# A four-layer decoder trunk: TensorE's instructions in the order of emission, with the emitter's clock and delays changed

## The chip, the cores and the metric

The kernel runs on 1 core of one Trainium2 chip. The metric is device time in microseconds (us) of one execution, and the median of the runs is what counts. TensorE does the products and transposes, VectorE, ScalarE and GpSimd the work between them, and SyncE issues most of the transfers.

## The reference

Four layers, 256 positions, model width 1024, all in float32. Layer i has mixer i mod 3 (so 0, 1, 2, 0) and a gated feed-forward block; each is wrapped in two RMS norms and added to x.

```python
for i in range(DEPTH):
    hn = rms_norm(x, norm_gains[i, 0])
    m = (diff_attention, stick_breaking_attention, sliding_window_sink_attention)[i % 3](hn, ...)
    x = x + rms_norm(m, norm_gains[i, 1])
    h = rms_norm(x, norm_gains[i, 2])
    f = (silu(h @ w_gate[i]) * (h @ w_up[i])) @ w_down[i]
    x = x + rms_norm(f, norm_gains[i, 3])
```

Each mixer projects hn to queries, keys and values, forms causal scores per head, turns them into weights (two softmaxes whose difference is taken; stick breaking; a softmax with a sink over a window of 128), applies them to the values and projects back. Mixers 0 and 2 rotate queries and keys by their positions (rope).

## The kernel before, in words

**Two streams.** The 256 positions are two streams of 128, stream 0 and stream 1. Both run the same layers, and stream 1 also needs the keys and values of stream 0. Every unit of weights (128 x 1024 floats, numbered in the order of use, `units`, L190 to L238) is used first by stream 0 and then by stream 1.

**Weights.** SyncE loads a unit into one of 4 staging tiles (`load_dma`, L242). ScalarE rounds it to `hi` and VectorE takes the rest as `lo` (`split`, L254); both are kept in a ring of 11. A product of float32 accuracy is three passes: hi by the high part of the activations, lo by the high part, hi by the low part. So a unit is six products of 512 columns for each stream in a mixer's projections, in the out-projection or in the feed-forward block.

**The parts of a layer.** `pre_norm` (L418) transposes x on TensorE and splits it into `xh` and `xl` (ScalarE, then VectorE, four slices for each half). `project` (L496) makes a chunk in a bank of PSUM: the first chunk of a mixer in an "acc" bank, the later ones in the one "mm" bank of the stream, which must have been read before the next chunk is written. In mixers 0 and 2 a chunk of queries or keys goes through `rope` (L510): two multiplications by VectorE that read the bank and an addition, then transposes (`tt`, `tq`, `tk`), then a copy by ScalarE. `scores` (L607 and L714) and `heads` (L807) make scores (`sc`), the weights, their transposes (`tw`, `ta`, `tpr`); `values` makes the output (`pv`), which mixer 0 normalises (`on`, with GpSimd's power) and transposes (`to`). `out_proj` (L483) is followed by `post_norm` (L457): squares by ScalarE, a power by GpSimd (`u_m`, then `r_m`), the update of x by VectorE. The feed-forward block (`ffn`, L871) has 11 chunks; a chunk's hidden values are turned by GpSimd copies and a transposing transfer (`hp`, `hq`, `hx` in `turn`, L891) and used by `down` (L880).

**What sets the order.** Each part is a generator. The `Emitter` (L42 to L155) runs them in turn and emits their instructions. It has a clock of its own, `t`, which only the products and transposes move on: `mm` (L374) adds the columns times `COLUMN_NS`, `transpose` (L386) four times as much for a column. A generator yields `("d", ns)` to be taken up again that much later by this clock, `("e", key)` to wait for an event of another part, and `("w",)` to ask for the next unit. Where nothing can be emitted, the clock jumps to the next due time. Small parts (transposes, scores, values) go first when they are due, then the two main generators.

What is emitted then goes to a scheduler that orders each engine's queue when the program is built. Instructions issued through `act`, `dve`, `pool` and `pe` (L187) are pinned behind what was emitted before them on their engine (`Start`, L172) as long as `on` is true. In the kernel before, all four are turned off at L933, when stream 1 has made its first norm of layer 0; from there on the scheduler chooses the order, and it may put a product of one part between two of another.

## Time and profile before

| | us |
|---|---|
| median of 3 runs | 1189.72 |
| lowest and highest | 1189.0, 1190.4 |
| the profiled execution's own time | 1188.92 |
| its span, first to last instruction | 1187.1 |

The profile is of one execution. Its page gives the busy time of each engine over the span; other views of the trace give it by stretch, list the instructions in order of time with start and length, and follow the chain of waits back from the end. A stretch is named by its start and end in us from the span's start. A group's name is what it writes, an arrow, and what it reads, with buffer numbers left out: `mm_f` is a feed-forward chunk, `mm_a010k` the key chunk of layer 0, stream 1, head group 0 (a for mixer 0, then layer, stream, group, part); `tp_q` are the transposes of x ahead of a feed-forward block and `tp_n` those ahead of a mixer; `acc` is an out-projection or down-projection. Layer 0's mixer lies from the start to 125, the feed-forward blocks of the four layers around 125 to 316, 420 to 610, 700 to 875 and 990 to the end.

### The profile page before, as it was taken

How to read it: one execution, taken by the hardware profiler on the slowest of the kernel's cores; microseconds unless marked ns; L12 is line 12 of the kernel's file. 1: busy time of each engine (PE TensorE's matmuls, PEld its weight loads, DVE VectorE, ACT ScalarE, POOL GpSimd, SP SyncE). 2: the span in 40 equal slices, each digit the busy share in tenths (PEclk: the TensorE clock that was granted, in tenths of full speed). 3: DMA queues.
4: the chain of work that ended last, by engine and by line, in shares of the span. 5: the costliest groups of instructions: out<-in, count | busy, mean ns of one | idle time of the engine just before them, and what ended most of it. 6: DMA issues, size and time to landing. Idle time of an engine off the chain costs nothing.

```text
span 1187.1 us, 16727 instructions
## 1 busy us (share of the span) xinstructions
PE 1165.9 (98%) x5868; PEld 958.5 (81%) x5868; DVE 784.4 (66%) x1217; ACT 651.9 (55%) x1197; POOL 214.3 (18%) x301
## 2 busy tenths in 40 slices
PE   8999999999999999999999999999999999999997
PEld 7787788888878878888888878888878788888886
DVE  7876665665847666665688666566586785666563
ACT  6665554444756655444476655445475565545442
POOL 2000132222200013222210013221210001322221
PEclk9999999999999999999999999999999999999999
DMA  7635467776743546777764246777765454677761
GB/s 280 212 122 161 146 189 222 209 213 199 239 143 125 178 143 185 216 219 209 200 214 141 90 147 195 213 210 210 207 214 154 137 175 128 177 213 214 208 194 41
DMA packets 184360, 216.41 MB, mean 182 GB/s; under 512 B 53074, under 2 KB 148436, under 8 KB 184276
## 3 DMA queue, kind: packets, MB, share of 16 engines
q1 hardware_dynamic: 183568, 215.00, 61.1%
q8 instruction: 46, 0.75, 0.3%
q10 hardware_dynamic: 708, 0.34, 0.1%
q14 instruction: 38, 0.31, 0.1%
HBM read 203.76 MB, written 1.05 MB: 173 GB/s over the span
## 4 chain that ended last, share of the span: by engine, by line
PE 90%; DVE 3%; ACT 3%; DMA 2%; issue 2%; POOL 1%; ACTq 0%; POOLq 0%; DVEq 0%; SPq 0%
PE mm_f L182 39%; PE acc_f L182 19%; PE acc_a L182 3%; PE mm_c L182 2%; PE acc_b L182 2%; PE sc_a L182 2%; PE acc_c L182 2%; DMA stage<-in_a_w_in_dram 1%; ACT hi L182 1%; DVE lo L182 1%; PE sc_c L182 1%; PE sc_b L182 1%; PE pv_a L182 1%; DVE x L182 1%; PE tp_q L182 1%
## 5 line engine op out<-in xcount | busy, mean ns | idle before, releaser
L182 DVE TENSOR_TENSOR lo<-stage,hi 128x1024 fp32r<-128x1024 f32 x378 | 459.7, 1226 | 162.0 <-ACT hi L182 159.9
L182 ACT ACTIVATE hi<-stage 128x1024 fp32r<-128x1024 f32 x378 | 394.9, 1056 | 163.3 <-PE mm_f L182 86.9
L182 PE MATMUL mm_f<-hi,xh_q 128*128 128x512 f32 x704 | 275.7, 392 | 1.5 <-ACT hi L182 1.5
L182 PE MATMUL mm_f<-lo,xh_q 128*128 128x512 f32 x704 | 274.2, 389 | 0.0
L182 PE MATMUL mm_f<-hi,xl_q 128*128 128x512 f32 x704 | 217.2, 390 | 0.4 <-DVE xl_q L182 0.4
L182 POOL COPY hp_f<-h_f 128x512 uint16<-128x512 uint16 x80 | 90.6, 1132 | 407.7 <-DVE h_f L182 393.7
L182 PEld LDWEIGHTS mm_f<-hi,xh_q 128*128 128x128 f32 x704 | 132.1, 188 | 30.5 <-ACT hi L182 3.2
L182 PEld LDWEIGHTS mm_f<-hi,xl_q 128*128 128x128 f32 x704 | 132.2, 188 | 28.7 <-DVE xl_q L182 1.2
L182 PEld LDWEIGHTS mm_f<-lo,xh_q 128*128 128x128 f32 x704 | 132.3, 188 | 26.9
L182 ACT ACTIVATE hTh_f<-hx_f 128x256 fp32r<-128x256 f32 x80 | 33.4, 418 | 166.8 <-POOL hx_f L182 166.8
L182 PE MATMUL acc_f<-hi,hTh_f 128*128 128x512 f32 x352 | 111.5, 393 | 1.2 <-ACT hTh_f L182 1.2
L182 PE MATMUL acc_f<-hi,hTl_f 128*128 128x512 f32 x352 | 109.8, 390 | 0.0
L182 PE MATMUL acc_f<-lo,hTh_f 128*128 128x512 f32 x352 | 109.8, 390 | 0.0
L182 DVE TENSOR_TENSOR hTl_f<-hx_f,hTh_f 128x256 fp32r<-128x256 f32 x80 | 33.9, 424 | 106.0 <-ACT hTh_f L182 106.0
L182 POOL COPY hx_f<-hq_f 128x512 uint16<-128x512 uint16 x80 | 81.0, 1013 | 85.6 <-DMA hq_f<-hp_f 85.1
L182 ACT ACTIVATE t_f<-mm_f,half_f 128x256 f32<-128x256 f32 x88 | 41.5, 472 | 74.4 <-PE mm_f L182 74.4
L182 PEld LDWEIGHTS acc_f<-hi,hTh_f 128*128 128x128 f32 x352 | 65.8, 188 | 15.5 <-ACT hTh_f L182 2.3
L182 PEld LDWEIGHTS acc_f<-lo,hTh_f 128*128 128x128 f32 x352 | 66.1, 188 | 13.8
L182 PEld LDWEIGHTS acc_f<-hi,hTl_f 128*128 128x128 f32 x352 | 66.0, 188 | 13.7
L182 DVE SCALAR_TENSOR_TENSOR t_f<-t_f,mm_f 128x256 f32<-128x256 f32 x88 | 36.8, 418 | 32.5 <-ACT t_f L182 32.4
L182 DVE SCALAR_TENSOR_TENSOR h_f<-t_f,hsq_f,mm_f 128x256 f32<-128x256 f32 x88 | 42.3, 480 | 2.9
L182 ACT ACTIVATE e_a<-sc_a,nm_a 128x128 f32<-128x128 f32 (+1 forms) x64 | 26.0, 420 | 17.0 <-DVE nm_a L182 16.9
(588 smaller groups left out, 1552.3 us busy)
## 6 DMA issues: line engine op xcount, KB each, us to landing
stage<-in_ffn_w_gate_dram SPq DMA_DIRECT2D x176, 256.0 KB, 3.0
stage<-in_ffn_w_up_dram SPq DMA_DIRECT2D x176, 256.0 KB, 3.3
stage<-in_ffn_w_down_dram SPq DMA_DIRECT2D x88, 512.0 KB, 4.4
stage<-in_a_w_in_dram SPq DMA_DIRECT2D x48, 512.0 KB, 4.4
stage<-in_b_w_in_dram SPq DMA_DIRECT2D x24, 512.0 KB, 4.1
stage<-in_a_w_out_dram SPq DMA_DIRECT2D x16, 512.0 KB, 3.5
stage<-in_c_w_in_dram SPq DMA_DIRECT2D x10, 512.0 KB, 4.4
gain<-in_norm_gains_dram SPq DMA_DIRECT2D x8, 512.0 KB, 4.3
```

What stands on the lines that cost most here:

```text
L182: i = call(*args, **kw)
```

## The change

TensorE's pin is no longer turned off, so its queue stands in the order of emission throughout; ScalarE, VectorE and GpSimd are let go at the same place as before. The clock's price of a column goes from 0.417 to 0.443 ns. The delays of nearly all parts are longer, and some yields are moved, taken out or added; two lines of them stand here for the table.

```diff
-COLUMN_NS = 1.0 / 2.4
+COLUMN_NS = 0.443
...
         def turned(chunk, g, which):
             t = rope(chunk, 8, *tabs[which], f"{name}{g}{which}")
-            yield ("d", 2000)
+            yield ("d", 2900)
...
-                    yield ("d", 3500)
+                    yield ("d", 1800 if step else 4200)
...
             split_rows(hT[c], slice(2 * (c % 2), 2 * (c % 2) + 2), t)
+            yield ("d", 1500)
             em.set((name, "h", c))
...
             if i == 0 and s:
                 scalars()
-                act.on = dve.on = pool.on = pe.on = False
+                act.on = dve.on = pool.on = False
...
             post_norm(s, acc, gain, f"m{i}{s}")
-            yield ("d", 4000)
+            yield ("d", 4600)
             gain = gain_of(i, 3)
             xn = pre_norm(s, 4 * i + 2, f"q{i}{s}")
-            yield ("d", 600)
+            yield ("d", 1200)
```

The instructions are the same ones before and after; only their order differs. In the rows below a name's last number is the buffer's and tells nothing; the number after hi or lo is the unit.

TensorE in layer 0, where the first query chunk of stream 0 (`t1_a000q`, after its rope) is transposed (`tt_a000q`). Before:

```order
L182 MATMUL mm_a000k_408<-hi_7_417,xh_n00_214 128x512
L182 MATMUL mm_a010q_359<-lo_3_293,xh_n01_297 128x512
L182 MATMUL mm_a000k_408<-lo_7_418,xh_n00_214 128x512
L182 MATMUL mm_a000k_408<-hi_7_417,xh_n00_214 128x512
L182 MATMUL mm_a000k_408<-lo_7_418,xh_n00_214 128x512
L182 MATMUL tt_a000q_402<-ident_164,t1_a000q_384 128x128 x4
L182 MATMUL mm_a000k_408<-hi_7_417,xl_n00_215 128x512 x2
```

After:

```order
L182 MATMUL mm_a010q_359<-hi_1_253,xl_n01_298 128x512 x2
L182 MATMUL mm_a000k_401<-hi_4_331,xh_n00_214 128x512
L182 MATMUL mm_a000k_401<-lo_4_332,xh_n00_214 128x512
L182 MATMUL mm_a000k_401<-hi_4_331,xh_n00_214 128x512
L182 MATMUL mm_a000k_401<-lo_4_332,xh_n00_214 128x512
L182 MATMUL mm_a000k_401<-hi_4_331,xl_n00_215 128x512 x2
L182 MATMUL tt_a000q_415<-ident_164,t1_a000q_384 128x128 x4
L182 MATMUL mm_a000k_401<-hi_5_368,xh_n00_214 128x512
```

The transposes stood among the products of unit 7; now they stand behind unit 4 of the key chunk, with units 0 and 1 for stream 1 ahead of that and units 5 to 7 behind. On VectorE, whose order is the same up to the rope's last addition, the splits of units 10 to 12 now stand ahead of the key chunk's rope, where only unit 10's stood within it; and later in this mixer `on_a000`, the normalisation of the first output, stands ahead of both multiplications that read the key chunk of stream 1, and before behind them.

TensorE at the entry of stream 1 into layer 0's feed-forward block (`x_1` is its x, `acc_a01` its out-projection, `mm_f00..` are chunks of stream 0 and `mm_f010` the first chunk of stream 1). Before:

```order
L182 MATMUL acc_a01_1_1326<-hi_31_1256,ol_a011_358 128x512
L182 MATMUL mm_f001_1469<-hi_39_1491,xh_q00_1362 128x512
L182 MATMUL mm_f001_1469<-lo_39_1492,xh_q00_1362 128x512
L182 MATMUL mm_f001_1469<-hi_39_1491,xh_q00_1362 128x512
L182 MATMUL mm_f001_1469<-lo_39_1492,xh_q00_1362 128x512
L182 MATMUL mm_f001_1469<-hi_39_1491,xl_q00_1363 128x512 x2
L182 MATMUL mm_f002_1661<-hi_42_1577,xh_q00_1362 128x512
L182 MATMUL acc_f00_0_1631<-hi_40_1514,hTh_f000_1557 128x512
L182 MATMUL tp_q01_0_1588<-ident_164,x_1_111 128x128 x4
L182 MATMUL acc_f00_1_1632<-hi_40_1514,hTh_f000_1557 128x512
L182 MATMUL tp_q01_1_1593<-ident_164,x_1_111 128x128 x4
L182 MATMUL mm_f010_1624<-hi_32_1275,xh_q01_1586 128x512
```

After:

```order
L182 MATMUL mm_f001_1469<-hi_39_1491,xl_q00_1369 128x512 x2
L182 MATMUL tp_q01_0_1588<-ident_164,x_1_111 128x128 x4
L182 MATMUL tp_q01_1_1593<-ident_164,x_1_111 128x128 x4
L182 MATMUL mm_f010_1624<-hi_32_1275,xh_q01_1586 128x512
L182 MATMUL mm_f010_1624<-lo_32_1276,xh_q01_1586 128x512
L182 MATMUL mm_f010_1624<-hi_32_1275,xh_q01_1586 128x512
L182 MATMUL mm_f010_1624<-lo_32_1276,xh_q01_1586 128x512
L182 MATMUL mm_f010_1624<-hi_32_1275,xl_q01_1587 128x512 x2
L182 MATMUL acc_f00_0_1635<-hi_40_1514,hTh_f000_1537 128x512
```

The products of units 42 and 40 that stood ahead of the transposes are behind them now; what stands ahead, up to `mm_f001`, is as before. GpSimd at the same place, before:

```order
L182 COPY hp_f000_1501<-h_f000_1465 128x512
L182 TENSOR_SCALAR u_m01_1549<-ssp_m01_1543 128x1
L182 COPY hx_f000_1559<-hq_f000_1503 128x2x256
L182 TENSOR_TENSOR r_m01_1550<-u_m01_1549,mhalf_126 128x1
L182 COPY hp_f001_1581<-h_f001_1570 128x512
```

After:

```order
L182 COPY hp_f000_1495<-h_f000_1465 128x512
L182 COPY hx_f000_1539<-hq_f000_1497 128x2x256
L182 TENSOR_SCALAR u_m01_1555<-ssp_m01_1549 128x1
L182 TENSOR_TENSOR r_m01_1556<-u_m01_1555,mhalf_126 128x1
L182 COPY hp_f001_1581<-h_f001_1570 128x512
```

The copy `hx_f000` stood between the two steps of stream 1's norm and now stands ahead of both. The entries of layers 1, 2 and 3 are changed in the same way on both engines.

TensorE in layer 2, where the keys of stream 0 are transposed (`tk_c20`, of `kd_c20` after its rope; `mm_c200` is the chunk that they come from, `mm_c201` the next). Before:

```order
L182 MATMUL mm_c201_6033<-lo_199_5963,xh_n20_5873 128x256
L182 MATMUL mm_c201_6033<-hi_199_5962,xl_n20_5874 128x256 x4
L182 MATMUL mm_c210_6087<-hi_196_5762,xh_n21_5999 128x256
L182 MATMUL tk_c20_5993<-ident_164,kd_c20_5984 128x128 x2
L182 MATMUL mm_c210_6087<-lo_196_5763,xh_n21_5999 128x256
```

After:

```order
L182 MATMUL mm_c200_5947<-lo_197_5785,xh_n20_5873 128x256
L182 MATMUL mm_c200_5947<-hi_197_5784,xl_n20_5874 128x256 x4
L182 MATMUL tk_c20_5993<-ident_164,kd_c20_5984 128x128 x2
L182 MATMUL tp_n21_0_6001<-ident_164,x_1_111 128x128 x4
L182 MATMUL tp_n21_1_6006<-ident_164,x_1_111 128x128 x4
L182 MATMUL mm_c201_6033<-hi_198_5816,xh_n20_5873 128x256
```

The key transposes stood behind the whole chunk `mm_c201` and the transposes of stream 1; now they stand directly behind the chunk that they need, ahead of both.

## The prediction

> **What bounds the kernel now.** First the page's busy times, then the busy time of each engine by stretch (columns: stretch, its length, then busy time and count of TensorE's matmuls, of its weight loads, of VectorE, ScalarE and GpSimd, the granted clock, the DMA share), cut at the mixers and feed-forward blocks.

> ```profile
> span 1187.1 us, 16727 instructions
> PE 1165.9 (98%) x5868; PEld 958.5 (81%) x5868; DVE 784.4 (66%) x1217; ACT 651.9 (55%) x1197; POOL 214.3 (18%) x301
> ...
> 0.00:40.00 40.00, 35.41 (x172) 29.13 (x173) 32.56 (x60) 25.80 (x39) 8.21 (x57) 1.00 0.79 272
> 40.00:125.00 85.00, 83.31 (x471) 67.03 (x470) 59.64 (x103) 52.75 (x146) 4.95 (x6) 1.00 0.48 150
> 125.00:150.00 25.00, 23.58 (x107) 18.62 (x106) 17.26 (x34) 14.56 (x30) 3.95 (x9) 1.00 0.52 158
> 150.00:290.00 140.00, 140.00 (x619) 116.04 (x618) 84.58 (x107) 65.79 (x87) 39.19 (x36) 1.00 0.74 208
> 610.00:700.00 90.00, 88.11 (x677) 75.12 (x676) 71.12 (x168) 60.05 (x167) 3.31 (x8) 1.00 0.44 141
> 875.00:990.00 115.00, 113.73 (x632) 92.37 (x631) 85.71 (x154) 71.48 (x185) 7.80 (x13) 1.00 0.49 155
> 1155.00:1187.10 32.10, 25.33 (x113) 20.35 (x111) 13.17 (x21) 7.36 (x16) 3.04 (x6) 0.95 0.12 42
> ```

> TensorE is the bound: it is idle for 1187.1 - 1165.9 = 21.2 us. Of that, 40.00 - 35.41 = 4.6 lie in the first 40 us and 32.10 - 25.33 = 6.8 in the last stretch, where the last norm and the store follow the last product; the order of TensorE's work shortens neither. So 9.8 us are left for a better order. Inside a feed-forward block (150 to 290) there is nothing: 140.00 of 140. Mixers 0, 2 and 3 hold 1.7, 1.9 and 1.3 us, and the entry of stream 1 into a feed-forward block (125 to 150) 1.4, four times over. The work itself is fixed, since the same instructions are issued before and after: what can change is only where TensorE waits. The chain of waits gives the pace, with which distances in an order become times:

> ```profile
> 172.11 8.16 PE mm_f L182 x36
> ```

> 36 products of 512 columns take 8.16 us, 0.227 each; six of them, one unit of weights for one stream, 1.36.

> An instruction at the head of TensorE's queue that waits holds all behind it, in either kernel. A place in the new order therefore costs the length of the chain on the other engines, by the trace, less the products that stand between. The five places where this comes out largest follow.

> **1. The first query transposes.** Rows of the timeline, start and length first:

> ```profile
> 19.74 0.39 PE L182 MATMUL mm_a010q<-hi,xh_n 128*128 128x512 f32 x1
> ...
> 25.82 0.68 DVE L182 TENSOR_TENSOR t_a000q<-mm_a000q,srq_a 128x512 f32<-128x512 f32 x1
> 26.43 1.21 DVE L182 TENSOR_TENSOR lo<-stage,hi 128x1024 fp32r<-128x1024 f32 x1
> 27.56 0.68 DVE L182 TENSOR_TENSOR t_a000q<-t_a000q 128x512 f32<-128x512 f32 x1
> ...
> 29.26 0.60 PE L182 MATMUL tt_a000q<-ident,t_a000q 128*128 128x128 f32 x4
> ```

> Stream 1's first products begin at 19.74, just behind the query chunk. Between that moment and the transposes the new order keeps 18 products (units 0 and 1 for stream 1, unit 4 for stream 0), so TensorE is at the transposes at 19.74 + 18 x 0.227 = 23.82. VectorE's order up to the rope's last addition is the same in both kernels, and that addition ends at 27.56 + 0.68 = 28.24. TensorE waits 4.4 us, give or take the 0.1 to 0.4 of a hand-over; before, products of units 2 to 7 filled this time. Nothing hides it, as the products that did stand behind the waiting transposes.

> **2. The value chunk behind it.** It uses the bank of the key chunk, which VectorE must have read twice. In the new order VectorE splits units 8 to 12 before the first of these two reads.

> ```profile
> 24.10 1.05 ACT L182 ACTIVATE hi<-stage 128x1024 fp32r<-128x1024 f32 x1
> ...
> 33.52 1.06 ACT L182 ACTIVATE hi<-stage 128x1024 fp32r<-128x1024 f32 x1 [0.40 <-DMA stage<-in_a_w_in_dram]
> ...
> 33.01 0.69 DVE L182 TENSOR_TENSOR t_a000k<-mm_a000k,srk_a 128x512 f32<-128x512 f32 x1
> ```

> The first of these ScalarE rows is unit 7, the second, five roundings later and waiting for its load, unit 12. VectorE's split of unit 12 can thus end at 33.52 + 1.06 + 1.21 = 35.8, the two reads at 0.6 each at 37.0. TensorE arrives at 28.3 + 0.4 + 30 x 0.227 = 35.5. That is 1.5 us; it is 0 if the loads run ahead during the first wait. Before, the second read ended at 33.70.

> **3. The middle of mixer 0.** VectorE's row of the normalised output of pv_a000 now stands ahead of both reads of the key chunk of stream 1, whose bank the value chunk needs.

> ```profile
> 52.30 0.28 ACT L182 ACTIVATE junk_a<-pv_a 128x128 bf16<-128x128 f32 x1 [1.16 <-PE pv_a L182]
> ...
> 54.80 0.69 DVE L182 TENSOR_TENSOR on_a<-pv_a,os_a 128x512 f32<-128x512 f32 x1 [1.16 <-POOL os_a L182]
> ...
> PE mm_a001k L182 <- DVE t_a001q L182: 0.7, 1, 0.7
> ```

> From pv_a's end (just before 52.30) to on_a's end is 3.2 us, and the two reads make it 4.4. Six products, 1.36, stand between: 3.0 us of wait. Before, TensorE waited 0.7 for a rope in this stretch (the last row: total, times, longest), which goes, and I take another 0.3 off for hand-overs beside it: +2.0, between 0 and 3.0.

> **4. Stream 1's entry into each feed-forward block**, four times.

> ```profile
> 141.81 0.39 PE L182 MATMUL acc_a<-hi,ol_a 128*128 128x512 f32 x1
> ...
> 143.02 0.30 POOL L182 TENSOR_SCALAR u_m<-ssp_m 128x1 f32<-128x1 f32 x1 [7.76 <-ACT junk_m L182]
> 143.38 0.75 POOL L182 COPY hx_f<-hq_f 128x512 uint16<-128x512 uint16 x1
> 143.92 0.49 PE L182 MATMUL mm_f<-hi,xh_q 128*128 128x512 f32 x1 [0.37 <-ACT hi L182]
> 144.07 0.57 POOL L182 TENSOR_TENSOR r_m<-u_m,mhalf 128x1 f32<-128x1 f32 x1
> ...
> 144.64 0.50 PE L182 MATMUL acc_f<-hi,hTh_f 128*128 128x512 f32 x1 [0.22 <-ACT hTh_f L182]
> 144.68 1.41 DVE L182 SCALAR_TENSOR_TENSOR x<-mg_m,r_m,x 128x512 f32<-128x512 f32 x2 [1.03 <-POOL r_m L182]
> ...
> 145.57 0.63 PE L182 MATMUL tp_q<-ident,x 128*128 128x128 f32 x4 [0.43 <-DVE x L182]
> ...
> 148.20 2.16 DVE L182 SCALAR_TENSOR_TENSOR xl_q<-tp_q,gains,xh_q 128x128 fp32r<-128x128 f32 x8
> ```

> Before: the last product of out-projection starts at 141.81, seven products later TensorE would be at 143.40. It waits three times, to 143.92, 144.64 and 145.57, and issues one product after each of the first two: 145.57 - 143.40 - 2 x 0.227 = 1.7 us lost. After: those two products are gone from here, so the transposes head the queue at 143.40. GpSimd's copy hx_f now stands ahead of u_m, so r_m starts at 143.32 instead of 144.07 and x comes 0.7 earlier: transposes at 144.85, a wait of 1.45. Their second half waits 0.35 for the second half of x. Then four products run, and the fifth needs xl_q, for which VectorE still has to do its queue behind x: in the trace 148.20 + 0.27 is 3.8 after x began, less the 0.3 of a subtraction that moved ahead gives 147.5, where TensorE stands ready at 146.86. Sum 1.45 + 0.35 + 0.65 = 2.45, or 0.75 more than before; four entries make +3.0. The copy that moved ahead costs nothing while its transfer has long landed; if that move gave nothing, x would come 0.7 later in all four, +5.8; if the three old waits merely merge into one, 0.

> **5. The keys of layer 2.** The transposes of the key chunk now stand right behind that chunk; before, 24 products of 256 columns, the transposes of stream 1 and a product lay between.

> ```profile
> 618.55 0.28 PE L182 MATMUL mm_c<-hi,xh_n 128*128 128x256 f32 x1
> ...
> 620.33 0.28 DVE L182 TENSOR_TENSOR t_c20k<-mm_c,srk_c 128x128 f32<-128x128 f32 x1
> ...
> 621.66 0.48 DVE L182 TENSOR_TENSOR kd_c<-t_c20k 128x128 f32<-128x128 f32 x2
> ```

> At 618.55 the chunk was done; the keys are ready at 622.14, and VectorE's order up to there is unchanged. The wait is 3.6 us, 2.4 if VectorE gets there without the split of 1.21 that stands between.

> **The rest.** Some six more places in mixers 2 and 3 have transposes directly behind a group that must be copied out of the same bank first. The gain elsewhere is at most the idle time of the three mixers, 1.7 + 1.9 + 1.3 = 4.9. The loss: such a copy and its subtraction cost

> ```profile
> 62.44 0.69 ACT L182 ACTIVATE oh_a<-to_a,gsub 128x512 fp32r<-128x512 f32 x1
> ...
> 63.66 0.74 DVE L182 SCALAR_TENSOR_TENSOR ol_a<-to_a,gsub,oh_a 128x512 fp32r<-128x512 f32 x1
> ```

> 0.69 + 0.74 = 1.4 each, at most 8 for six. I take the middle of -4.9 and +8, +1.5, as no row decides. SyncE's queue keeps its order but for one transposing transfer in layer 2, so the loads cost nothing by themselves; TensorE's longer delays between groups come free in the feed-forward blocks, where 140 of 140 us stay filled.

> **Sum.** 4.4 + 1.5 + 2.0 + 3.0 + 3.6 + 1.5 = +16.0 on the profiled execution's 1188.92 (its span of 1187.1 and 1.8 around it): 1204.9. The median of the three runs, 1189.72, lies 0.8 above that execution, so 1205.7, or 1206. With every term at its low end (4.0, 0, 0, 0, 2.4, -4.9) it is +1.5, 1191; at its high end (4.5, 1.5, 3.0, 5.8, 3.6, 8) +26.4, 1216.

> **The rivals.**

> *The clock falls during the long waits* (chance 0.12). In the trace TensorE never idles for long after the start, and at the start it is slow:

> ```profile
> 12.32 1.05 PE L182 MATMUL mm_a000q<-hi,xl_n 128*128 128x512 f32 x2
> 13.17 1.91 PE L182 MATMUL tp_n<-ident,x 128*128 128x128 f32 x8
> ```

> Two products take 13.17 - 12.32 = 0.85, twice the later pace. If waits 1 and 5 each brought back such a stretch, and it lasted as long as from there to 19.74 at most, each would cost up to half of 6.6 us, 3.3: 1206 + 6.6 = 1213. For it: two waits of 4 us, longer than any of before. Against it: the granted clock is given as 1.00 in all stretches but the last, so the page can't tell.
> [...]

> *The chains stay as long as in the trace everywhere* (0.15). The other engines' orders change little, so every rope that queued behind splits there may queue in the new order too, and hold TensorE at each group. All terms are then at their high ends, 1216, and with four ropes more at the 1.5 of place 2, 1222.

> *The waits of before go, and the new ones are short* (0.08): the other side, faster. VectorE's three operations for a rope are 0.68 each, 2.0 in all; where it is free at once, the distances in the new order cover them. Then terms 2, 3 and the rest turn into -4.9, and the entries gain their 0.7: 4 x (-0.7). It decides at the startup, in VectorE's addition: were it done by 23.8, wait 1 would be gone too, and with wait 5 halved the time is 1189.7 - 4.9 - 2.8 + 1.8 = 1183.8. Against it: VectorE's queue up to there is the same, and full, so I see no way to its being done before 28.

> *Nothing measurable* (0.05): the old and new waits cancel, 1190. It needs wait 1 and wait 5, 8 us, to be made good by 8 of the 9.8 idle us, which include the entries.

> The forecast has 0.60. **How the numbers follow.** 0.2%, about what a measurement of this kernel can tell from no change, is 2.4 us. The first, second and forecast cases are slower: 0.87; the third faster, 0.08; the fourth the same, 0.05. The range goes from 1194, leaving out the last two cases and the very lowest sum, to 1222, the end of the long-chain case.

> **What would show it.** In the profile after: TensorE waits on VectorE's t_a000q for some 4 us around 24, on kd_c for some 3.6 around 630, and on x before each tp_q of stream 1 for 1.4; mm_f in the blocks keeps 0.227. Wrong would be: no wait at tt_a000q or tk_c, or idle time of TensorE below 21 us. Products at twice the pace behind a wait would speak for the clock.

## The result, and the profile after

The changed kernel takes 1224.12 us (median of 4 runs, 1222.58 to 1225.83), the kernel before 1189.36 beside it: ratio 1.029, 95% interval 1.0277 to 1.0303. The profiled execution took 1222.58. Its page, the busy times:

```profile
span 1220.8 us, 16727 instructions
PE 1173.2 (96%) x5868; PEld 961.7 (79%) x5868; DVE 787.2 (64%) x1217; ACT 654.3 (54%) x1197; POOL 214.0 (18%) x301
```

TensorE is idle for 1220.8 - 1173.2 = 47.6 us, 26.4 more than before, and busy 7.3 us longer with the same 5868 instructions: together the 33.7 us by which the span has grown. The stretches show where (columns as before; the granted clock stands behind the five busy times):

```profile
0.00:40.00 40.00, 31.32 (x135) 25.24 (x136) 31.07 (x56) 24.21 (x33) 8.23 (x57) 0.91 0.80 281
40.00:137.00 97.00, 90.32 (x515) 72.94 (x514) 63.09 (x111) 56.49 (x152) 5.76 (x8) 0.98 0.40 122
162.00:300.00 138.00, 138.00 (x611) 114.26 (x610) 82.31 (x101) 64.30 (x84) 38.00 (x35) 1.00 0.72 205
627.00:716.00 89.00, 80.15 (x620) 68.56 (x621) 62.67 (x152) 54.81 (x156) 3.46 (x8) 0.96 0.33 108
905.00:1024.00 119.00, 111.90 (x616) 90.75 (x617) 83.33 (x150) 70.61 (x183) 7.38 (x12) 0.99 0.46 141
```

Inside a feed-forward block nothing is lost, as before. Mixers 0, 2 and 3 hold 6.7 (and 8.7 in the first 40 us), 8.9 and 7.1 us of idle time, and the clock is below 1 in just these stretches. The list of TensorE's waits (total, times, longest) gives them their names:

```profile
PE tp_q L182 <- DVE x L182: 5.4, 4, 1.4
PE tt_a000q L182 <- DVE t_a000q L182: 4.0, 1, 4.0
PE mm_a010v L182 <- DVE t_a010k L182: 3.4, 1, 3.4
PE tk_c L182 <- DVE kd_c L182: 3.0, 2, 2.7
PE tt_a301q L182 <- DVE ol_a L182: 2.8, 1, 2.8
PE tpr_c L182 <- ACT pT_c L182: 2.3, 2, 1.7
PE mm_a311k L182 <- DVE t_a311q L182: 2.2, 1, 2.2
PE mm_a011k L182 <- DVE t_a011q L182: 2.2, 1, 2.2
```

The four largest are the prediction's places 4, 1, 3 and 5; the others are not on its list. The timeline at place 1 shows both halves of a loss, the wait and what follows it:

```profile
23.86 0.63 PE L182 MATMUL mm_a000k<-hi,xl_n 128*128 128x512 f32 x2
28.44 1.11 PE L182 MATMUL tt_a000q<-ident,t_a000q 128*128 128x128 f32 x4 [3.96 <-DVE t_a000q L182]
...
30.21 0.63 PE L182 MATMUL mm_a000k<-hi,xh_n 128*128 128x512 f32 x1
30.64 0.63 PE L182 MATMUL mm_a000k<-lo,xh_n 128*128 128x512 f32 x1
```

Behind the wait the products start 0.43 apart instead of 0.227; the granted clock is 0.50 from 26.52 to 33.35. And the entry of stream 1 into layer 0's feed-forward block:

```profile
155.39 1.23 PE L182 MATMUL tp_q<-ident,x 128*128 128x128 f32 x8 [1.36 <-DVE x L182]
...
158.08 0.76 PE L182 MATMUL mm_f<-hi,xl_q 128*128 128x512 f32 x2 [0.41 <-DVE xl_q L182]
```

1.36 + 0.41 = 1.77 of waiting, where the rows of before have 0.37 + 0.22 + 0.43 = 1.02. Layers 1 and 3 wait as long as layer 0 to 0.02, before and after; in layer 2 the kernel before had waited 0.37 + 1.15 = 1.52 already.

### The profile page after: what moved, and what is told of

Read it like the earlier page. It is cut to its first block, busy times and chain, and to the rows that moved or that the text cites. A ratio compares the mean times of both kernels' runs of the same rounds, so it can differ in the third digit from the quotient of the medians.

```text
span 1220.8 us, 16727 instructions
## 1 busy us (share of the span) xinstructions
PE 1173.2 (96%) x5868; PEld 961.7 (79%) x5868; DVE 787.2 (64%) x1217; ACT 654.3 (54%) x1197; POOL 214.0 (18%) x301
## 3 DMA queue, kind: packets, MB, share of 16 engines
HBM read 203.76 MB, written 1.05 MB: 168 GB/s over the span
## 4 chain that ended last, share of the span: by engine, by line
PE 78%; DVE 5%; ACT 3%; issue 1%; DMA 1%; POOL 1%; DVEq 0%; POOLq 0%; ACTq 0%; SPq 0%
PE mm_f L182 38%; PE acc_f L182 18%; DVE lo L182 2%; PE acc_b L182 2%; PE acc_a L182 2%; PE acc_c L182 1%; ACT hi L182 1%; PE mm_c L182 1%; DVE x L182 1%; ACT e_c L182 1%; PE sc_b L182 1%; PE sc_a L182 1%; PE mm_a311k L182 1%; PE pv_b L182 0%; PE mm_a311q L182 0%
## 5 line engine op out<-in xcount | busy, mean ns | idle before, releaser
L182 DVE TENSOR_TENSOR lo<-stage,hi 128x1024 fp32r<-128x1024 f32 x378 | 459.7, 1227 | 179.5 <-ACT hi L182 178.0
L182 ACT ACTIVATE hi<-stage 128x1024 fp32r<-128x1024 f32 x378 | 395.7, 1058 | 183.2 <-PE mm_f L182 94.1
L182 PE MATMUL mm_f<-hi,xh_q 128*128 128x512 f32 x704 | 274.9, 390 | 0.0
L182 PE MATMUL mm_f<-lo,xh_q 128*128 128x512 f32 x704 | 273.9, 389 | 0.0
L182 PE MATMUL mm_f<-hi,xl_q 128*128 128x512 f32 x704 | 217.8, 390 | 2.0 <-DVE xl_q L182 1.9
L182 POOL COPY hp_f<-h_f 128x512 uint16<-128x512 uint16 x80 | 91.1, 1138 | 417.5 <-DVE h_f L182 406.9
L182 PEld LDWEIGHTS mm_f<-hi,xl_q 128*128 128x128 f32 x704 | 132.1, 188 | 32.6 <-DVE xl_q L182 5.0
L182 PEld LDWEIGHTS mm_f<-hi,xh_q 128*128 128x128 f32 x704 | 132.1, 188 | 27.6 <-ACT xh_q L182 0.2
L182 PEld LDWEIGHTS mm_f<-lo,xh_q 128*128 128x128 f32 x704 | 132.2, 188 | 27.2
L182 ACT ACTIVATE hTh_f<-hx_f 128x256 fp32r<-128x256 f32 x80 | 33.6, 419 | 163.0 <-POOL hx_f L182 163.0
L182 PE MATMUL acc_f<-hi,hTl_f 128*128 128x512 f32 x352 | 110.0, 390 | 1.6 <-DVE hTl_f L182 1.6
L182 PE MATMUL acc_f<-hi,hTh_f 128*128 128x512 f32 x352 | 110.1, 390 | 0.5 <-ACT hTh_f L182 0.5
L182 PE MATMUL acc_f<-lo,hTh_f 128*128 128x512 f32 x352 | 109.8, 389 | 0.0
L182 DVE TENSOR_TENSOR hTl_f<-hx_f,hTh_f 128x256 fp32r<-128x256 f32 x80 | 33.9, 424 | 102.6 <-ACT hTh_f L182 102.6
L182 POOL COPY hx_f<-hq_f 128x512 uint16<-128x512 uint16 x80 | 80.5, 1006 | 95.8 <-DMA hq_f<-hp_f 95.6
L182 ACT ACTIVATE t_f<-mm_f,half_f 128x256 f32<-128x256 f32 x88 | 41.6, 473 | 85.3 <-PE mm_f L182 85.3
L182 PEld LDWEIGHTS acc_f<-hi,hTl_f 128*128 128x128 f32 x352 | 65.9, 188 | 16.2 <-DVE hTl_f L182 2.5
L182 PEld LDWEIGHTS acc_f<-lo,hTh_f 128*128 128x128 f32 x352 | 66.1, 188 | 13.8
L182 PEld LDWEIGHTS acc_f<-hi,hTh_f 128*128 128x128 f32 x352 | 65.8, 188 | 14.1 <-ACT hTh_f L182 0.8
L182 DVE SCALAR_TENSOR_TENSOR t_f<-t_f,mm_f 128x256 f32<-128x256 f32 x88 | 36.8, 418 | 39.3 <-ACT t_f L182 39.3
L182 DVE SCALAR_TENSOR_TENSOR h_f<-t_f,hsq_f,mm_f 128x256 f32<-128x256 f32 x88 | 42.3, 480 | 2.9
L182 POOL TENSOR_TENSOR os_a<-os_a,mhalf 128x4 f32<-128x4 f32 x8 | 8.1, 1017 | 166.0 <-DVE os_a L182 166.0
```

Source lines behind the costliest of these rows:

```text
L182: i = call(*args, **kw)
```

## The experiments

All times are medians; the ratios are to runs of the kernel before on the same chip (medians from 1189.36 to 1189.80). For each kernel the length of its layers tells where a loss lies: from the first transposes of a layer's norm (`tp_n`) to those of the next, layer 0 from the start and layer 3 to the end of the last product.

| kernel | time | ratio, 95% | layer 0 | 1 | 2 | 3 |
|---|---|---|---|---|---|---|
| before | 1189.36 | 1 | 312.5 | 298.6 | 266.1 | 303.6 |
| changed | 1224.12 | 1.0277 to 1.0303 | 323.8 | 300.6 | 278.4 | 311.8 |
| pin, old delays | 1231.13 | 1.0332 to 1.0396 | 328.9 | 301.8 | 280.9 | 311.1 |
| free, new delays | 1189.07 | 0.9985 to 1.0005 | 313.8 | 297.9 | 264.6 | 304.5 |
| pin in feed-forward only | 1197.21 | 1.0046 to 1.0076 | 316.1 | 299.7 | 267.1 | 306.3 |
| pin in mixers only | 1217.41 | 1.0216 to 1.025 | 324.3 | 298.3 | 275.4 | 309.8 |
| products in order, parts free | 1206.13 | 1.0117 to 1.0157 | 321.6 | 299.3 | 270.0 | 308.7 |
| waits filled | 1220.34 | 1.0242 to 1.0272 | 324.2 | 300.2 | 275.8 | 311.6 |
| two places moved | 1227.52 | 1.0303 to 1.0335 | 323.3 | 301.1 | 283.8 | 311.6 |
| longer behind q and k | 1232.21 | 1.0346 to 1.0377 | 332.2 | 300.2 | 275.7 | 315.2 |
| all engines pinned | 1271.11 | 1.0674 to 1.0703 | 335.8 | 303.4 | 305.9 | 320.4 |
| column price in feed-forward | 1184.90 | 0.9949 to 0.9974 | 312.3 | 297.5 | 264.6 | 302.2 |
| the same and delays of 1, 2 | 1185.12 | 0.9951 to 0.9976 | 312.1 | 298.0 | 263.7 | 302.7 |

The theory: the loss is the pin, through TensorE's waits at the head of a fixed order and the half clock behind the long ones. The rivals: the longer delays cost; the clock is the larger part; or TensorE's order only clashes with orders that the scheduler gives the other engines.

**Pin or delays.** Two kernels make one half of the change each. Pin alone, on the kernel before:

```diff
-                act.on = dve.on = pool.on = pe.on = False
+                act.on = dve.on = pool.on = False
```

> The kernel before with TensorE's pin kept, and nothing else changed: clock and delays are the old, shorter ones. Theory: a fixed order pays for every chain on VectorE, ScalarE and GpSimd that is longer than the distance given to it; the old delays give shorter distances than the new, so the time is well over that of the kernel before, 1215 to 1240 us, and not better than that of the changed kernel (1224). Rival, the longer delays and the new clock are what costs: about 1190. If the pin is the cause but the new delays do nothing useful: 1224.

Clock and delays alone, on the changed kernel, is the same line the other way:

```diff
-                act.on = dve.on = pool.on = False
+                act.on = dve.on = pool.on = pe.on = False
```

> The changed kernel with TensorE's pin let go where it was before: new clock and new delays, and the scheduler chooses TensorE's order. Theory: the scheduler fills the places, so 1186 to 1194 us, within some 4 us of the kernel before. Rival, the delays and the clock are what costs: 1215 to 1225.

Measured: 1231.13 and 1189.07. The pin is the loss, 41.5 us with the old delays and, against the second kernel, 35.1 with the new; the delays give 7 of it back. By themselves they cost nothing in sum, and the rival of the delays has fallen. The sum hides two sides, though: without the pin, layers 0 and 3 are 1.3 and 0.9 longer than before and layers 1 and 2 are 0.7 and 1.5 shorter. The largest wait left in this free kernel is the one of place 3:

```profile
PE mm_a010v L182 <- DVE t_a010k L182: 3.0, 1, 3.0
```

The kernel with the pin alone has no wait there. So it comes with VectorE's order under the new delays, where `on_a000` stands ahead of both reads, as the prediction had it, and not with the pin.

**Where the pin costs.** On the changed kernel, the pin switched by the place of stream 0: first on in the feed-forward blocks only, then the opposite.

```diff
+            if i and not s:
+                pe.on = False
             xn = pre_norm(s, 4 * i, f"n{i}{s}")
...
-                act.on = dve.on = pool.on = False
+                act.on = dve.on = pool.on = pe.on = False
...
+            if not s:
+                pe.on = True
             post_norm(s, acc, gain, f"m{i}{s}")
```

> The changed kernel with TensorE's pin let go in the four mixers and kept from stream 0's entry into each feed-forward block to its exit. Theory: the loss of the changed kernel is 3 us at the entries of stream 1 and some 30 in the mixers, so 1190 to 1195 us. Rival, a fixed order costs wherever it holds, also by what it leaves to the next mixer: 1205 or more.

```diff
+            if i and not s:
+                pe.on = True
             xn = pre_norm(s, 4 * i, f"n{i}{s}")
...
+            if not s:
+                pe.on = False
             post_norm(s, acc, gain, f"m{i}{s}")
```

> The opposite: the pin kept in the mixers and let go from stream 0's entry into each feed-forward block to its exit. Theory: 1217 to 1223 us, 1 to 7 less than the changed kernel. Rival as before: 1210 or less.

Measured: 1197.21 and 1217.41. Against the free kernel with the new delays (1189.07) these are +8.1 and +28.3, 36.5 together, beside 35.1 for the pin everywhere: the two add up, and three quarters lie in the mixers. The first came out 2 above its range, because I had set the entries against the kernel before, which loses 1.7 at each, and the right base loses 0.5 there, as the column price further down shows.

**Which instructions.** Only the large products are kept in order among themselves; transposes, scores and value products are free.

```diff
-                act.on = dve.on = pool.on = False
+                act.on = dve.on = pool.on = pe.on = False
...
-        pe.matmul(o, a, b, start=start, stop=stop)
+        i = pe.matmul(o, a, b, start=start, stop=stop)
+        if not f32 and a is not identb:
+            if behind and not pe.on:
+                tc.add_manual_dep(i.ins, behind[0].ins.name, mybir.DependencyInfo(
+                    mybir.DependencyClass.NoSync, mybir.DependencyReason.DATA), reason="order of the products")
+            behind[:] = [i]
```

> The changed kernel with only the products of the projections, of the out-projections and of the feed-forward blocks in their order among themselves; the transposes, scores and value products are left to the scheduler. Theory: what costs is that a small part at the head of the queue holds the products behind it, so with the small parts free 1188 to 1196 us. Rival, the order of the products, with which stream's unit comes when, costs: 1210 or more.

Measured: 1206.13, between the two answers, so each takes about half: 17 for the order of the products, 18 for the fixed place of the small parts. What waits are left:

```profile
PE tp_q L182 <- DVE x L182: 5.4, 4, 1.4
PE mm_a010v L182 <- DVE t_a010k L182: 3.0, 1, 3.0
PE mm_a000v L182 <- DVE t_a000k L182: 2.2, 1, 2.2
PE mm_a011k L182 <- DVE t_a011q L182: 2.0, 1, 2.0
PE mm_a311k L182 <- DVE t_a311q L182: 2.0, 1, 2.0
```

The entries, and chunks that wait for the one bank which VectorE's rope has not yet read. Freeing the transposes does not help these, and the second of them, 3.0 at `mm_a010v`, is in the kernel that is all free too.

**The half clock by itself.** Products with no use, whose results are overwritten, keep TensorE at work through the waits at places 1 and 5.

```diff
-    def four_transposes(s, src, dst, name):
+    def four_transposes(s, src, dst, name, fill=0):
...
+        for _ in range(fill):
+            pe.matmul(tp, identb, identb.unsqueeze(1).to_broadcast([P, 4, P]), start=True, stop=True)
...
+            fill = 16 if (name, g, which) == ("a00", 0, "q") else 0
...
+            for _ in range(0 if s else 22):
+                pe.matmul(tp, identb, identb.unsqueeze(1).to_broadcast([P, 2, P]), start=True, stop=True)
```

> The changed kernel with extra products, whose results are overwritten, ahead of the transposes of the first query chunk of stream 0 (16 of 512 columns) and of the first key chunk of layer 2 (22 of 256 columns), so that TensorE works through these two waits of 4.1 and 2.9 us and still cannot go on before the operands are there. Theory: both stretches of half clock behind them go (6.8 us each in the changed kernel), the waits themselves stay: 4 to 6 us less than the changed kernel, 1218 to 1220. If the half clock costs nothing, as other waits absorb it: 1224. If the clock is the larger part of the loss: below 1210.

Measured: 1220.34, 3.8 less, just short of what was expected. Behind the filled wait the pace is whole:

```profile
24.06 3.63 PE L182 MATMUL tt_a000q<-identb 128*128 128x512 bf16 x16
28.18 0.66 PE L182 MATMUL tt_a000q<-ident,t_a000q 128*128 128x128 f32 x4 [0.49 <-DVE t_a000q L182]
...
28.91 0.39 PE L182 MATMUL mm_a000k<-lo,xh_n 128*128 128x512 f32 x1
29.14 0.40 PE L182 MATMUL mm_a000k<-hi,xh_n 128*128 128x512 f32 x1
```

Layer 2 is 2.6 shorter, layer 0 not at all. It is ahead for a while: the chunk `mm_a000v` starts at 35.98, in the changed kernel at 38.08. The granted clock is 0.994 over this run and 0.990 over the changed kernel, which without its two stretches of 6.83 us at half clock would have 0.996 (half of 13.66 in 1220.8 is 0.0056). So half clock came up elsewhere, by an estimate from the difference of 0.002 some 2 us of lost time, and the 3.8 are what is left of the gain. At which wait it came, and how much of layer 0's lead it took, these figures do not show. The clock is a real but minor part: TensorE is longer busy by 7.3 us in the changed kernel, of 33.7 lost. How much of the waits a whole clock everywhere would change was not measured.

**Mending places one by one.** First the two longest waits, by letting more work stand ahead of them:

```diff
-            yield ("d", 2900)
+            yield ("d", 8000 if (name, g, which) == ("a00", 0, "q") else 2900)
...
-            yield ("d", 2300)
+            yield ("d", 2300 if part else 0)
```

> The changed kernel with two delays altered: 8000 for 2900 ahead of the first query transposes of stream 0 in layer 0, so that most of the startup's free products stand ahead of them, and 0 for 2300 behind the first half of stream 0's chunk in layer 2, so that 24 products of 256 columns stand ahead of its key transposes. Theory: the waits of 4.1 and 2.9 us fall below 1 us and the half clock behind them goes with them: 10 to 13 us less than the changed kernel, 1211 to 1214. If what is saved at a place is only waited for at the next one: 1220 or more.

Measured: 1227.52, 3.4 more: a miss, and the theory that a place can be priced and mended by itself fell with it. Both waits are gone, and others stand in their place (list of waits):

```profile
PE mm_a000v L182 <- DVE t_a000k L182: 3.4, 1, 3.4
...
PE tt_a001q L182 <- DVE ol_a L182: 2.6, 1, 2.6
PE acc_c L182 <- ACT e_c L182: 2.6, 1, 2.6
PE tq_c L182 <- ACT pT_c L182: 2.5, 3, 1.0
PE tq_c L182 <- DVE ol_c L182: 2.1, 1, 2.1
```

In the startup a reason can be seen. The stretch from 20 to 36 of the kernel before:

```profile
20.00:36.00 16.00, 16.00 (x76) 13.30 (x75) 15.13 (x23) 11.23 (x13) 3.71 (x6) 1.00 0.75 246
```

and of this experiment:

```profile
20.00:36.00 16.00, 11.44 (x50) 8.30 (x49) 14.07 (x22) 10.79 (x12) 3.75 (x6) 0.99 0.73 230
```

VectorE is nearly full in both, and frees the key chunk's bank at about 34 in both. The kernel before issues 76 instructions of TensorE meanwhile, the fixed order 50: it runs out of work that may go, at one instruction or the next. For layer 2, where this run lost 5.4, no such reason was found.

Second, more time behind each query and key chunk of mixers 0 and 3, so that the next chunk finds the bank free:

```diff
-                    yield ("d", 2200)
+                    yield ("d", 4500)
```

> The changed kernel with 4500 for 2200 behind each query and key chunk of mixers 0 and 3, so that units of the other stream, or none, stand ahead of the next chunk in the same bank. The run with the products alone in order has left three waits of products on that bank in mixer 0. Theory: the waits there of 3.6, 2.4 and 0.7 us (in mixers 0 and 3 twice) and two stretches of half clock go, 1210 to 1216. If the wait is passed on to the next place, as in the run with two places moved: 1221 or more.

Measured: 1232.21, 8 more, a miss again. The long waits on the bank are gone. The wait at `tt_a000q` is a little longer than its 4.0 in the changed kernel, and other transposes wait for their ropes:

```profile
PE tt_a000q L182 <- DVE t_a000q L182: 4.3, 1, 4.3
PE tt_a310k L182 <- DVE t_a310k L182: 3.5, 1, 3.5
PE tt_a010k L182 <- DVE t_a010k L182: 3.5, 1, 3.5
...
PE tt_a000k L182 <- DVE t_a000k L182: 2.7, 1, 2.7
```

**Are the other engines' orders at fault?** All four engines stay pinned (the first norm keeps its own form, which hung on the same switch).

```diff
-                act.on = dve.on = pool.on = False
...
-        if act.on:
+        if n == 0:
```

> The changed kernel with VectorE, ScalarE and GpSimd kept in the order of emission throughout as well. The run with two places moved has shown that relieving one wait of TensorE only brings out the next one behind it, so something beside TensorE's order may set the time there. If that is the mismatch between TensorE's order and the orders that the scheduler gives the other engines: 1210 or less. If the chains themselves are longer than the distances that the delays give, whoever orders them: 1220 or more.

Measured: 1271.11. In this form the rival of clashing orders has fallen: with the other engines in the order of emission TensorE waits longer still (4.9 at `tk_c`, where it waited 2.7, and 4.5 at `mm_a011k` instead of 2.2). Another order of VectorE, made to suit the fixed order of TensorE, was not tried.

**A version that is faster than both.** In the free kernel with the new delays, one part was better than before: at the entries TensorE lost 0.5 instead of 1.7. The order shows that this comes from the column price, which puts five products of the down-projection ahead of or between the transposes. So, on the kernel before, only this, and only in the feed-forward blocks:

```diff
+            if not s:
+                em.column = COLUMN_NS
             xn = pre_norm(s, 4 * i, f"n{i}{s}")
...
+            if not s:
+                em.column = 0.443
             post_norm(s, acc, gain, f"m{i}{s}")
```

with `em.column` in place of `COLUMN_NS` in `mm` and `transpose`.

> The kernel before, all free, where only the clock's price of a column is 0.443 ns from stream 0's entry into a feed-forward block to its exit, and 0.417 elsewhere: the orders in the mixers are those of before, and five products of the down-projection stand ahead of stream 1's first transposes. In the free kernel with the new delays TensorE loses 0.5 us at this place where the kernel before loses 1.7. Theory: four entries times 1.2, 4.7 us less than the kernel before, 1184 to 1186. If the products that fill the wait are missing later: 1189 to 1190.

The second kernel adds the new delays of all parts but mixers 0 and 3.

> The same, and the new delays everywhere but in mixers 0 and 3, whose order stays that of the kernel before. In the free kernel with the new delays, layers 1 and 2 came out 0.7 and 1.5 us shorter than before, entries included. Theory: as the run above, within 1 us, 1183.5 to 1186, since mixers 1 and 2 had little to gain. If the new delays cost there: above 1187.

Measured: 1184.90 and 1185.12, both as expected. The entry of the first (its lines are one further down):

```profile
144.33 0.61 PE L183 MATMUL acc_f<-hi,hTh_f 128*128 128x512 f32 x2
144.78 0.61 PE L183 MATMUL acc_f<-lo,hTh_f 128*128 128x512 f32 x2
145.75 0.66 PE L183 MATMUL tp_q<-ident,x 128*128 128x128 f32 x4 [0.36 <-DVE x L183]
```

4.7 us are what the kernel before could gain at this place, and the delays add nothing to it.

## Why the prediction was wrong in size

The direction held, and so did the mechanism at places 1, 3, 4 and 5: TensorE waits there for the chains that were named. But 33.7 us were lost between first and last instruction where the sum had 16.0. By its steps:

1. First query transposes, +4.4: 3.96 of waiting, right.
2. The bank behind it, +1.5: no wait. VectorE's reads ended at 37.6 (foreseen 37.0), but TensorE, at half clock, came later, at 38.1. That is luck: the sum had no half clock, and the prediction's reason for a 0 here was another, loads that run ahead.
3. Middle of mixer 0, +2.0: the wait itself is 3.41 (foreseen 3.0). But layer 0 lost 11.3 in all; less 4.0 at place 1 and 0.75 at the entry that leaves 6.6 for its middle. The wait of 2.2 at `mm_a011k` and the half clock (0.50 from 64.07 to 67.48, behind the wait of 3.41) were not in the sum. This wait of 3.41 is the one that comes with the delays: 3.0 without the pin, and none with the pin alone.
4. Entries, +0.75 each: 1.77 - 1.02 = 0.75 in layers 0, 1 and 3, right, with GpSimd's copy out of the way as foreseen. In layer 2 it is 1.77 - 1.52 = 0.25, since the sum took one entry of before for all four.
5. Keys of layer 2, +3.6: 2.69 of waiting, near the low end of 2.4, and then 2.7 for the clock (shown in the last section). The low end had VectorE without the split that stands between; the split still stood there, and VectorE came to the reads 0.8 us behind the chunk instead of 1.6.

**"The rest", +1.5, is the step that failed.** Less entries and place 5, layer 1 lost 2.0 - 0.75 = 1.3, layer 2 12.3 - 0.25 - 5.4 = 6.6, layer 3 8.1 - 0.75 = 7.4: 15.3, outside its bounds of -4.9 and +8. I had priced six places at one copy and one subtraction, 1.4 each, and taken the middle to a gain that no row supported. But mixer 3 has the parts of mixer 0, and the same waits on ropes, such as 2.2 at `mm_a311k` beside 2.2 at `mm_a011k`; steps 2 and 3 price waits on ropes at 1.5 and 3.0 for mixer 0, and none is priced for mixer 3. Nor is 1.4 the price of a copy and its subtraction: ahead of `tt_a301q` they take 0.67 and 0.75, but the copy ends at 951.06 and the subtraction begins at 952.26, behind a split of 1.23 and a rope's addition of 0.69 in VectorE's queue, and TensorE waits 2.8. And in mixer 2 it is the chain from one bank through ScalarE's copies to the next instruction of TensorE: the list of waits has 2.3, 1.2, 0.8 and 0.2 on `pT_c` and `e_c` in the changed kernel, 4.5 of the 6.6, and none on them before.

The rival of the clock, kept out of the sum with a chance of 0.12, came true beside the forecast, not in place of it: the prediction took as alternatives what adds up. The rival of long chains everywhere (1216 to 1222) came nearest and was still 2 too low; it left out the half clock, which cost 2.7 in layer 2 alone. The rival of short waits failed where it was said to be decided: VectorE's addition ended at 28.4, not by 23.8.

What stays open is the rest of the 6.6 of layer 2, and why moving one place there cost 5.4 more (layer 2, 283.8 against 278.4): I can name the waits that came but not why they are more.

## What to carry to other kernels

Price an in-order queue over whole stages, not by its few worst places. In two runs here a wait that was mended came out at other instructions; where another engine is nearly full beside the queue, as VectorE in this startup (15.13 us busy of 16.00 in the kernel before, 14.07 with two places moved), only more work that may go meanwhile would, as I read these two runs, take it away. Before pinning a queue, run the pin and the delays apart; here the one useful part of the change was a single price in four places, worth 0.4%, hidden under a loss of 2.9%. Where a chain is priced for one block, use that price for every block of the same kind.

## What the runs showed of the hardware

```profile
630.68:634.09 3.41, 1.46 (x13) 1.26 (x11) 3.41 (x7) 3.12 (x4) 0.37 (x1) 1.00 0.78 273
634.09:637.51 3.42, 2.67 (x13) 2.68 (x14) 2.66 (x9) 2.05 (x9) 0.93 (x2) 0.50 0.49 172
637.51:640.92 3.41, 3.41 (x18) 3.41 (x18) 3.11 (x9) 1.08 (x5) 0.00 (x0) 0.50 0.66 222
```

then in the other:

```profile
638.03:641.45 3.42, 2.13 (x18) 1.93 (x17) 3.42 (x9) 3.13 (x4) 0.87 (x2) 1.00 0.75 280
641.45:644.86 3.41, 2.02 (x18) 2.02 (x19) 2.65 (x8) 2.71 (x9) 0.92 (x2) 1.00 0.62 177
644.86:648.27 3.41, 3.41 (x31) 3.41 (x30) 3.41 (x9) 1.06 (x5) 0.00 (x0) 1.00 0.67 211
```

In the first the wait falls mostly into one stretch, which is idle to 1.95 / 3.41 = 57%, and two at half clock follow. In the second it lies across two, idle to 38% and 41%, and the clock stays at 1.00; layer 2, the same in both, is 278.4 - 275.7 = 2.7 us shorter. In the changed kernel the 3.41 us ahead of the four falls were idle to 60%, 57%, 57% and 66%; of the other stretches of that length at full clock, counted on from these and between the first 20 us and the end, the most idle had 50.4% (688.70 to 692.11). So a wait of 2.2 us (at `mm_a311k`, 985 us) was followed by half clock, and one of 2.8 (at `tt_a301q`, 953 us, across two stretches idle to 37% and 45%) was not. That it is the place of a wait among these stretches that decides is my reading of these places; no run tested it, and for the second kernel no row shows a fall in step with its three stretches.
